# Compressed keys of layer 1: two full-array fp32r products of high and low rows in place of two fp32 products of 15 rows

## Chip, cores and metric

The kernel runs on 1 core of one Trainium2 chip. The metric is the device time of one launch in microseconds (us), lower is better. The time of a kernel is the median of several runs; one further execution is taken with the hardware profiler, and all rows below are of that one.

## What is computed

The reference is two layers of a decoder on one sequence of 256 positions with 1024 channels. Each layer is RMS norm, attention, output projection, residual; then a SwiGLU block with 2816 hidden channels; then a gated per-layer embedding. Layer 0 has two kinds of local attention and isn't touched here. Layer 1 has 16 query heads in 4 groups, each group with its own keys and values, and three branches that are summed with sigmoid gates:

```python
s = jnp.einsum('bghsd,bgcd->bghsc', qg, kc).astype(F32) * ATTN_SCALE + tabg[:, :, _rel_bucket(dc)].astype(F32)
p_cmp, _ = _masked_softmax(s, dc >= 0)
o_cmp = jnp.einsum('bghsc,bgcd->bghsd', p_cmp.astype(vc.dtype), vc)
...
o = (gates[..., 0:1] * o_cmp.reshape(B, H, S, hd) + gates[..., 1:2] * o_slc.reshape(B, H, S, hd)
     + gates[..., 2:3] * o_win.reshape(B, H, S, hd))
```

Here `kc` and `vc` are the compressed keys and values: windows of 32 positions with a stride of 16, each put through a small two-layer network. A sequence of 256 gives 15 of them for each group. The change concerns the product `o_cmp`, of the weights over these 15 compressed keys (`p_cmp`) with their values.

## The kernel before

Everything is fp32 in memory. The large products are made of fp32r products: each weight tile is split by ScalarE (a rounded copy `hi`, L135) and VectorE or GpSimd (the rest `lo`, L137), the activations likewise into the x tiles, `X[0]` and `X[1]`, which hold for each of 8 rows of 128 channels a high and a low part of 256 positions. Three products (high by high, low by high, high by low) stand for one of fp32. The attention of both layers works with plain fp32 for the softmax weights and the values.

TensorE's and the load queue's (SP) instructions run in the order in which the program writes them; the other engines' order is left to the framework's scheduler. The program's order comes from a planner. Every product adds its price to a clock `clk` (`mm`, L148 to L153): the larger of moving and stationary columns over 2400 us, times 4 for fp32, times 0.56 if the product has only 64 stationary columns or 64 rows. Side jobs (generators) give out their next step once the clock has reached their due time, between two chunks of the large products (`tick`, `side_step`). The constants in `KN` are due times and distances in this clock.

In layer 1 these side jobs run beside the projections for q, k and v, then `ple_proj` (tile `pa`) and the output projection (`oc`):

- `compress` (from L935) makes the compressed keys and values. Its second step copies the hidden values of each group into 4 blocks of 32 columns (L989), so that the product with the second weight leaves the values `VC` four times along the partitions, one copy at rows 0, 32, 64 and 96.
- `cmp_scores(b)`, once for each half `b` of the heads (two groups), makes the scores against the 15 compressed keys (`cs`), the softmax (L1035 to L1044), and writes the weights into `PC` with 32 columns for a head, of which 15 are used (L1046, two VectorE products). Four transposes (`pcp`) and one ScalarE copy (L1053) bring them to `PCT`, with 4 heads along the partitions.
- `attend` drives, for each half, the steps A (scores `s`, softmax with L498, L1082, L1083 to L1087), B (transposes `t`, copies to `pt`, L1097 and L1099) and C. C(k) is run 4 times for each half, once for a pair of heads: the heads `j` of the two groups.

C opens with the two products of the compressed branch, one for each head `e` of the pair, 15 rows and 64 columns of the stationary operand each:

```python
for e in range(2):
    mm(o[64 * e:64 * e + 64, 0:256], VC[32 * j:32 * j + 15, gs[e], :],
                     PCT[32 * j:32 * j + 15, gs[e], :], start=True, stop=False)
```

Then it adds the eight fp32 products of the other two branches with the values (`o<-pt`), and `o_evac` (L494, L495) brings the tile `o` into row `h0 // 2 + k` of `X[1]`, high part by ScalarE and low part by VectorE. The output projection reads `X[1]` two rows at a time (`out_proj`). When it is done, its result goes into `h` (L518) and, normalised, into a new `X[0]` (L412, L413).

`PCT` shares memory with `KCV`, the projected inputs of `compress`. `X[0]` holds the input of layer 1's projections and isn't read after the last of them. The memory of `X[1]` holds the first weight of `compress` (`w1`) until that has been used.

Of the kernel before, what the change touches and what calls it, by code (L numbers as in the profile page):

```python
# [39 lines left out]
def trunk(ctx: ExitStack, tc: tile.TileContext, a, out):  # L40
# [108 lines left out]
    def mm(o, l, r, start, stop):  # L149
        n, m = int(np.prod(r.shape[1:])), l.shape[-1]  # L150
        f = 1.0 if l.dtype == F32R else 4.0
        clk[0] += f * max(n, m) / 2400 * (0.56 if m == 64 or l.shape[0] == 64 else 1.0)
        nc.tensor.matmul(o, l, r, start=start, stop=stop)  # L153
# [703 lines left out]
    PCT = big2[:, 1536:2560].rearrange("p (g s) -> p g s", g=4)  # L857
    VC = big2[:, 2560:2816].rearrange("p (g d) -> p g d", g=4)
    G = big2[:, 2816:2912].rearrange("p (t h b) -> p t h b", t=2, h=16)
# [77 lines left out]
    def compress(idr):  # L937
# [44 lines left out]
        atvv = atv.rearrange("p (g r c) -> p g r c", g=4, r=4)  # L982
# [5 lines left out]
        for g in range(4):  # L988
            nc.vector.tensor_copy(atvv[:, g, :, 0:15], p[:, 64 + g * 15:79 + g * 15][:, None, :].to_broadcast([128, 4, 15]))  # L989
# [19 lines left out]
        for e in range(2):  # L1009
            ph, kh, gh = p[64 * e:64 * e + 64], KCT[64 * e:64 * e + 64, :, e], g[64 * e:64 * e + 64]  # L1010
            pv = bass.AP(tensor=ph.tensor, offset=ph.offset + 15 * e, ap=[ph.ap[0], [30, 2], [1, 16]])
            nc.scalar.activation(kh[:, :, 0, :], pv, AF.Identity, scale=gh)
            nc.vector.scalar_tensor_tensor(kh[:, :, 1, :], pv, gh, kh[:, :, 0, :].bitcast(F32), op0=OP.mult, op1=OP.subtract)
        ev["kc"] = clk[0] + 0.8

    def cmp_scores(b):
        if b == 0:
            nc.gpsimd.memset(PC, 0.0)
# [25 lines left out]
        nc.vector.tensor_tensor(l, l, G[:, :, 8 * b:8 * b + 8, 0], op=OP.mult)  # L1044
        for t in range(2):
            nc.vector.tensor_tensor(PC[:, t, :, 0:15], sc[:, t], l[:, t, :, None].to_broadcast([128, 8, 15]), op=OP.mult)  # L1046
# [6 lines left out]
        nc.scalar.activation(PCT[:, 2 * b:2 * b + 2, :], p.rearrange("p (a s) -> p a s", a=2), AF.Copy)  # L1053
        ev[f"cmp{b}"] = clk[0] + 0.8

    def attn1(h0):
# [45 lines left out]
        def C(k):  # L1102
# [3 lines left out]
            for e in range(2):  # L1106
                mm(o[64 * e:64 * e + 64, 0:256], VC[32 * j:32 * j + 15, gs[e], :],
                                 PCT[32 * j:32 * j + 15, gs[e], :], start=True, stop=False)
# [34 lines left out]
    new_x(1)  # L1143
# [77 lines left out]
```

## Time and profile before

| | |
|---|---|
| median of 3 runs | 715.0 us (711.7 to 715.34) |
| profiled execution, its own time | 709.85 us |
| its span, first to last instruction | 708.0 us |
| TensorE (PE) busy | 691.6 us, 98% |
| VectorE (DVE) busy | 509.2 us, 72% |
| ScalarE (ACT) busy | 411.6 us, 58% |
| GpSimd (POOL) busy | 179.4 us, 25% |

In the trace, times are counted from the span's start. An instruction is named by its engine, its line in the kernel, its operation and the tiles it writes and reads; "x4" is a number of instructions that stand in one row. A matmul's duration holds its way through the array, and consecutive ones overlap, so what a matmul costs in a row of many is read from the distance between starts. An fp32 matmul leaves two records. A note in brackets at the end of a row is the time that the engine stood idle before it, and what ended that. The chain of work that ended last is followed back from the last instruction: at each step to what released it, or to the instruction before it on its engine.

### The profile page before, as it was taken

What the parts mean: (1) busy time and instruction counts of PE and PEld (TensorE: products, weight loads), DVE (VectorE), ACT (ScalarE), POOL (GpSimd) and SP (SyncE); (2) the same over time, 40 slices, a digit from 0 to 9 for tenths busy, and PEclk for the clock granted to TensorE, in tenths of its full rate; (3) what the DMA queues carried; (4) which work ended last, traced back from release to release, by engine and by line L of the source; (5) the groups of instructions that cost most, each with busy time, mean ns of one, the idle gap of its engine ahead of it and who ended that gap; (6) DMA issues with size and microseconds to landing.
All of it is one profiled execution on the core that took longest, in us unless ns stands there. A gap on an engine that the chain in (4) does not pass through costs nothing.

```text
span 708.0 us, 12005 instructions
## 1 busy us (share of the span) xinstructions
PE 691.6 (98%) x4394; PEld 597.2 (84%) x4394; DVE 509.2 (72%) x973; ACT 411.6 (58%) x761; POOL 179.4 (25%) x287
## 2 busy tenths in 40 slices
PE   8999999999999999999999999998999999999996
PEld 6887789898888888899878867787988888888896
DVE  6669674878867765767876887766697778757465
ACT  7557685655665653554654777776465656645342
POOL 1353100242132220001163544341232321310010
PEclk9999999999999999999999999999999999999999
DMA  8956424556556565547763253622567555654611
GB/s 313 322 177 220 161 96 125 149 174 209 183 175 218 172 205 199 185 152 230 216 218 121 87 150 97 173 61 90 150 185 226 165 198 169 217 191 167 209 60 60
DMA packets 69931, 121.66 MB, mean 172 GB/s; under 512 B 5488, under 2 KB 17648, under 8 KB 69872
## 3 DMA queue, kind: packets, MB, share of 16 engines
q1 hardware_dynamic: 69872, 120.89, 53.6%
q8 instruction: 34, 0.56, 0.3%
q14 instruction: 25, 0.20, 0.1%
HBM read 119.83 MB, written 1.05 MB: 171 GB/s over the span
## 4 chain that ended last, share of the span: by engine, by line
PE 79%; DVE 7%; ACT 5%; POOL 4%; issue 3%; DMA 2%; SPq 0%; DVEq 0%; ACTq 0%; POOLq 0%
PE ua L153 17%; PE ga L153 17%; PE da L153 17%; PE oc L153 5%; PE ic L153 5%; PE pc L153 5%; DVE lo L137 3%; PE o L153 3%; ACT hi L135 2%; PE q L153 2%; PE s L153 2%; PE t L157 1%; PE v L153 1%; DMA raw<-in_w_in_nsa_dram 1%; PE pa L153 1%
## 5 line engine op out<-in xcount | busy, mean ns | idle before, releaser
L137 DVE TENSOR_TENSOR lo<-raw,hi 128x1024 fp32r<-128x1024 f32 (+2 forms) x218 | 265.7, 1230 | 106.4 <-ACT hi L135 106.1
L135 ACT ACTIVATE hi<-raw 128x1024 fp32r<-128x1024 f32 (+4 forms) x231 | 223.8, 987 | 159.3 <-PE da L153 50.7
L153 PE MATMUL ua<-x,hi 128*128 128x512 f32 (+1 forms) x384 | 96.1, 375 | 0.0
L153 PE MATMUL ga<-x,hi 128*128 128x512 f32 x352 | 92.9, 395 | 2.3 <-DVE h L518 1.8
L153 PE MATMUL da<-big,hi 128*128 128x512 f32 x352 | 89.6, 393 | 0.0
L153 PE MATMUL ic<-hi,x 128*128 128x512 f32 (+2 forms) x256 | 78.6, 376 | 0.1
L153 PEld LDWEIGHTS ua<-x,hi 128*128 128x128 f32 x384 | 65.9, 189 | 8.7
L153 PEld LDWEIGHTS ga<-x,hi 128*128 128x128 f32 x352 | 61.6, 189 | 12.8 <-DVE h L518 2.6
L153 PEld LDWEIGHTS da<-big,hi 128*128 128x128 f32 x352 | 62.7, 189 | 10.7
L601 POOL TENSOR_TENSOR th<-th,rfb 128x512 f32<-128x512 f32 x22 | 28.5, 1295 | 127.1 <-DVE th L600 127.1
L425 POOL TENSOR_TENSOR sum<-sum,sqj 128x512 f32<-128x512 f32 x12 | 17.1, 1422 | 171.2 <-ACT sqj L423 171.1
L153 PE MATMUL ua<-x,lo 128*128 128x256 f32 x352 | 57.1, 282 | 0.0
L153 PEld LDWEIGHTS ua<-x,lo 128*128 128x128 f32 x352 | 52.7, 189 | 5.1
L153 PEld LDWEIGHTS ga<-x,lo 128*128 128x128 f32 x352 | 51.0, 189 | 5.5
L153 PEld LDWEIGHTS ic<-hi,x 128*128 128x128 f32 x256 | 46.6, 188 | 10.2 <-issue 2.1
L153 PEld LDWEIGHTS da<-big,lo 128*128 128x128 f32 x352 | 49.1, 190 | 4.2
L153 PE MATMUL ga<-x,lo 128*128 128x256 f32 x352 | 52.5, 281 | 0.0
L153 PE MATMUL da<-big,lo 128*128 128x256 f32 x352 | 50.3, 282 | 0.0
L153 PE MATMUL oc<-x,hi 128*128 128x256 f32 x256 | 48.5, 289 | 0.1
L153 PE MATMUL ic<-lo,x 128*128 128x512 f32 (+2 forms) x128 | 46.9, 366 | 0.0
L153 PE MATMUL pc<-x,hi 128*128 128x256 f32 x256 | 46.6, 284 | 0.0
L610 POOL TENSOR_TENSOR th<-us,th 128x512 f32<-128x512 f32 x20 | 36.3, 1817 | 37.9 <-DVE us L568 37.9
(199 smaller groups left out, 1131.5 us busy)
## 6 DMA issues: line engine op xcount, KB each, us to landing
raw<-in_w_ffn_gate_dram SPq DMA_DIRECT2D x44, 512.0 KB, 3.7
raw<-in_w_ffn_up_dram SPq DMA_DIRECT2D x44, 512.0 KB, 4.4
raw<-in_w_ffn_down_dram SPq DMA_DIRECT2D x44, 512.0 KB, 3.8
raw<-in_w_in_ab_dram SPq DMA_DIRECT2D x23, 512.0 KB, 5.8
raw<-in_w_ple_gate_dram SPq DMA_DIRECT2D x16, 512.0 KB, 4.0
raw<-in_w_in_nsa_dram SPq DMA_DIRECT2D x12, 512.0 KB, 4.8
raw<-in_w_out_ab_dram SPq DMA_DIRECT2D x8, 512.0 KB, 3.3
raw<-in_w_in_nsa_dram SPq DMA_DIRECT2D x16, 256.0 KB, 3.8
```

Source lines behind the costliest of these rows:

```text
L135: nc.scalar.activation(hi[:, x:x + m], r[:, x:x + m], AF.Copy)
L137: e.tensor_tensor(lo[:, x:x + m], r[:, x:x + m], hi[:, x:x + m].bitcast(F32), op=OP.subtract)
L153: nc.tensor.matmul(o, l, r, start=start, stop=stop)
L157: nc.tensor.transpose(o, i, ident if idn is None else idn)
L425: e.tensor_tensor(st["sum"], st["sum"], j, op=OP.add)
L601: nc.gpsimd.tensor_tensor(v2(th), v2(th), r2(), op=OP.mult)
L610: nc.gpsimd.tensor_tensor(y, x, y, op=OP.mult)
```

## The change

The weights of the 15 compressed keys and their values are split into high and low parts, as the large products' operands are. The high and the low part of a head's weights lie side by side, at columns 0 to 14 and 16 to 30 of its 32, so that after the transposes a head has 32 rows: 15 high, one zero, 15 low, one zero. The values stand eight times along the partitions (blocks of 16) instead of four times, so that both the high and the low rows of a head meet the same values. For each pair of heads a stationary operand of 128 rows is built in which all but the pair's rows are zero: columns 0 to 63 hold the values of the first group in the rows of the pair's first head, columns 64 to 127 those of the second group in the rows of the second head. To that end `PC` is ordered by pairs (`p (j e) c`), and a mask `msk`, one column for each block of 32 rows, multiplies `VC` (`vc_blocks`). C then opens with two products over all 128 rows and 128 columns, with the high and with the low part of the values.

The new tiles have no memory of their own. For the first half of the heads they lie in rows 5 to 7 of `X[1]`, for the second in rows 5 to 7 of `X[0]` (`cmp_homes`). `new_x(1)` moves from the code after the projections into the end of `compress`.

```diff
-    PCT = big2[:, 1536:2560].rearrange("p (g s) -> p g s", g=4)
     VC = big2[:, 2560:2816].rearrange("p (g d) -> p g d", g=4)
+    PCR, VCR, PHR = {}, {}, {}
+    msk = small("msk", (128, 4))
+    nc.vector.tensor_reduce(msk, ident.rearrange("p (s c) -> p s c", c=32), axis=AX.X, op=OP.add)
+
+    def cmp_homes(b):
+        x = X[1 - b].rearrange("p k e s -> p k (e s)")
+        PCR[b] = x[:, 7].rearrange("p (q s) -> p q s", q=2)
+        VCR[b] = x[:, 6].rearrange("p (l n) -> p l n", l=2)
+        PHR[b] = x[:, 5, 0:240]
+
+    def vc_blocks(b):
+        w = wk_tile("vcw")[:, 0:256].rearrange("p (j e d) -> p j e d", j=2, e=2)
+        for j in range(2):
+            nc.vector.tensor_tensor(w[:, j], VC[:, 2 * b:2 * b + 2, :], msk[:, 2 * j:2 * j + 2][:, :, None].to_broadcast([128, 2, 64]),
+                                    op=OP.mult)
+        wf = w.rearrange("p j e d -> p (j e d)")
+        nc.scalar.activation(VCR[b][:, 0], wf, AF.Copy)
+        nc.vector.tensor_tensor(VCR[b][:, 1], wf, VCR[b][:, 0].bitcast(F32), op=OP.subtract)
...
-        atvv = atv.rearrange("p (g r c) -> p g r c", g=4, r=4)
+        atvv = atv.rearrange("p (g r c) -> p g r c", g=4, r=8)
...
-            nc.vector.tensor_copy(atvv[:, g, :, 0:15], p[:, 64 + g * 15:79 + g * 15][:, None, :].to_broadcast([128, 4, 15]))
+            nc.vector.tensor_copy(atvv[:, g, :, 0:15], p[:, 64 + g * 15:79 + g * 15][:, None, :].to_broadcast([128, 8, 15]))
...
+        new_x(1)
+        cmp_homes(0)
+        vc_blocks(0)
         ev["kc"] = clk[0] + 0.8

     def cmp_scores(b):
+        if b:
+            cmp_homes(1)
...
+        nc.vector.tensor_tensor(sc, sc, l[:, :, :, None].to_broadcast([128, 2, 8, 15]), op=OP.mult)
+        nc.scalar.activation(PHR[b], w[:, 0:240], AF.Copy)
+        ph = PHR[b].bitcast(F32).rearrange("p (t e j c) -> p t e j c", t=2, e=2, j=4)
+        sv = w[:, 0:240].rearrange("p (t e j c) -> p t e j c", t=2, e=2, j=4)
         for t in range(2):
-            nc.vector.tensor_tensor(PC[:, t, :, 0:15], sc[:, t], l[:, t, :, None].to_broadcast([128, 8, 15]), op=OP.mult)
+            pc = PC[:, t].rearrange("p (j e) c -> p e j c", e=2)
+            nc.vector.tensor_tensor(pc[:, :, :, 16:31], sv[:, t], ph[:, t], op=OP.subtract)
+            nc.scalar.activation(pc[:, :, :, 0:15], ph[:, t], AF.Copy)
+        if b:
+            vc_blocks(b)
         yield KN["cmp"]
...
-        nc.scalar.activation(PCT[:, 2 * b:2 * b + 2, :], p.rearrange("p (a s) -> p a s", a=2), AF.Copy)
+        nc.scalar.activation(PCR[b], p.rearrange("p (a s) -> p a s", a=2), AF.Copy)
...
-            for e in range(2):
-                mm(o[64 * e:64 * e + 64, 0:256], VC[32 * j:32 * j + 15, gs[e], :],
-                                 PCT[32 * j:32 * j + 15, gs[e], :], start=True, stop=False)
+            b = h0 // 8
+            for l in range(2):
+                mm(o[:, 0:256], VCR[b][:, l, 128 * (j % 2):128 * (j % 2) + 128], PCR[b][:, j // 2], start=l == 0, stop=False)
...
-    new_x(1)
```

## Rows read from the trace of the kernel before

**Rows 1.** The page, part 2: granted TensorE clock in 40 slices

```profile
PEclk9999999999999999999999999999999999999999
```

**Rows 2.** Busy time by stretch: PE, PEld, DVE, ACT, POOL, clock, DMA

```profile
397.50:437.30 39.80, 36.75 (x255) 28.50 (x254) 32.43 (x119) 30.14 (x91) 17.56 (x29) 1.00 0.38 100
437.30:452.35 15.05, 14.12 (x113) 11.07 (x113) 11.17 (x52) 9.99 (x33) 6.05 (x9) 1.00 0.69 194
452.35:485.60 33.25, 33.02 (x278) 25.64 (x278) 21.40 (x89) 22.68 (x71) 9.53 (x13) 1.00 0.27 80
```

**Rows 3.** Timeline of PE around the first C: start, us, instruction

```profile
419.74 0.40 PE L153 MATMUL pa<-px,hi 128*128 128x256 f32 x2
419.98 0.28 PE L153 MATMUL pa<-px,lo 128*128 128x256 f32 x1
420.18 0.65 PE L153 MATMUL o<-big 15*64 15x256 f32 x4
420.76 1.52 PE L153 MATMUL o<-pt,big 128*64 128x256 f32 x16
```

**Rows 4.** Busy time of PE in C's eight opening pairs, summed

```profile
sum 4.63, PE 4.62; mean PE 0.58
```

**Rows 5.** The chain that ended last, by time: start, us, work

```profile
428.15 1.18 POOL rs_tq L396
...
441.69 2.03 PE o L153 x20
...
445.84 0.77 ACT big L1082 x4
...
452.35 2.10 PE o L153 x20
...
482.64 2.05 PE o L153 x20
```

**Rows 6.** Groups by shape, 340 to 495 us, DVE, ACT: busy, mean ns

```profile
L1039 DVE TENSOR_TENSOR csw<-csw,cm 128x240 f32<-128x240 f32 x2 | 0.8, 404 | 0.0
...
L989 DVE COPY at<-atp 128x60 f32<-128x60 f32 x4 | 0.6, 210 | 0.0
...
L435 DVE TENSOR_TENSOR sum<-sum 128x256 f32<-128x256 f32 x1 | 0.4, 424 | 0.0
...
L135 ACT ACTIVATE hi<-raw 128x256 fp32r<-128x256 f32 x4 | 1.5, 420 | 1.0 <-issue 1.0
...
L1040 ACT ACTIVATE csw<-csw 128x240 f32<-128x240 f32 x2 | 0.8, 396 | 0.2 <-DVE csw L1039 0.2
...
L977 ACT ACTIVATE big<-big 128x128 f32<-128x128 f32 x1 | 0.3, 312 | 0.0
```

**Rows 7.** Timeline of DVE, first half of the heads, then the second

```profile
409.52 1.56 DVE L1046 TENSOR_TENSOR big<-csw,cl 128x120 f32<-128x120 f32 x2
...
413.97 1.23 DVE L137 TENSOR_TENSOR lo<-raw,hi 128x1024 fp32r<-128x1024 f32 x1 [0.86 <-ACT hi L135]
...
446.74 0.45 DVE L1046 TENSOR_TENSOR big<-csw,cl 128x120 f32<-128x120 f32 x2
...
447.97 0.69 DVE L137 TENSOR_TENSOR lo<-raw,hi 128x512 fp32r<-128x512 f32 x1 [0.70 <-ACT hi L135]
```

**Rows 8.** Timeline of POOL at the same two places

```profile
408.98 1.77 POOL L137 TENSOR_TENSOR lo<-raw,hi 128x512 fp32r<-128x512 f32 x1 [4.97 <-ACT hi L135]
...
447.43 2.86 POOL L1087 TENSOR_SCALAR big<-big,rl 128x128 f32<-128x128 f32 x4 [8.19 <-DVE rl L1085]
```

**Rows 9.** Timeline of ACT, second half of the heads

```profile
447.30 1.16 ACT L135 ACTIVATE hi<-raw 128x512 fp32r<-128x512 f32 x2 [0.69 <-issue]
449.10 0.51 ACT L1082 ACTIVATE big<-big,nm 128x256 f32<-128x256 f32 x1 [0.63 <-DVE nm L498]
```

**Rows 10.** Timeline of PE: the transposes of the weights, both halves

```profile
413.14 0.60 PE L157 MATMUL pcp<-ident,big 128*128 128x128 f32 x4
...
450.54 0.60 PE L157 MATMUL pcp<-ident,big 128*128 128x128 f32 x4
```

## The prediction

> **What bounds the kernel now.** I read the page's slices first, for the clock. TensorE is granted 90% of its clock or more in every slice [rows 1] and 1.00 in the stretches that matter here [rows 2], the higher of its two levels, 2.4 GHz; so a product costs the same wherever it stands, and nothing here is won or lost by the clock. Next came the busy time by stretch, cut where the attention of layer 1 changes character [rows 2]. From 397.5 to 437.3 us TensorE is busy 36.75 of 39.80 us, from 437.3 to 452.35 us 14.12 of 15.05, and from 452.35 to 485.6 us 33.02 of 33.25. So the last stretch is bound by TensorE alone, while the first two hold 3.05 + 0.93 = 4.0 us in which it stands idle. Then came the chain that ended last [rows 5], for the question whether TensorE also sets the time where the changed products stand. It does so from 452.35 us on. Before that the chain changes hands: at 428.15 us it runs over GpSimd while TensorE has other work, at 441.69 us it is on TensorE, from 445.84 us on ScalarE, and back on TensorE at 452.35 us. VectorE and ScalarE are no bound by their sums (11.17 and 9.99 of 15.05 us in the middle stretch), but they carry the chain there.
>
> **The change, part by part.**
>
> *The products.* Step C of a pair of heads opens with two fp32 products of 15 rows, which leave four records. The first starts at 420.18 us, and the products with the values (o<-pt) follow at 420.76: 0.58 us [rows 3]. Over the eight pairs it is 4.63 us, 0.58 each [rows 4]. In their place come two fp32r products of 128 rows, 128 stationary columns and 256 moving ones. That is the shape and type of the pa products just before: two start at 419.74 us and the next at 419.98, so 0.12 us each with their weight loads [rows 3]. The new pair costs 0.24 us, and C gets shorter by 0.58 - 0.24 = 0.34 us, eight times 2.7 us. One thing the rows leave open is the change from a full-array fp32r product to an fp32 one on part of the array. From the last pa product to the first 15-row one it took 0.20 us instead of 0.12, so 0.08 more. I take it that this gap then stands in front of o<-pt instead; if it falls away a pair saves 0.42 us, if it comes twice 0.26. All eight then lie between 2.1 and 3.4 us.
>
> *What of it is on the path.* Six of the eight groups are pieces of the chain: those at 441.69 and 452.35 us, three between there and the last, and the last at 482.64 [rows 5]. The first two, the one at 420.18 us and the next, are not: the chain passes through ScalarE, VectorE and GpSimd then, as at 428.15 us; what they save becomes a longer wait of TensorE a few us on. So 6 x 0.34 = 2.0 us counts (1.6 to 2.5).
>
> *More work for VectorE and ScalarE, once for each half of the heads.* Before, two VectorE products wrote the weights of the compressed keys. After, one 128x240 product takes their place (0.40 us, as L1039 [rows 6]), ScalarE rounds it (0.40, as L1040), VectorE subtracts twice (the pair at 446.74 us has that size, 0.45 [rows 7]) and ScalarE copies the high parts twice (0.31 each, as L977). The masked values add two VectorE products of 128x128 (0.46, taken from the same pair), a ScalarE copy of 128x256 (0.42, as L135 of that shape) and a VectorE subtraction (0.42, as L435). VectorE: 0.40 + 0.45 + 0.46 + 0.42 less the 0.45 removed is 1.28 us. ScalarE: 0.40 + 0.62 + 0.42 is 1.44 us.
>
> For the first half there is cover. The old pair ends at 409.52 + 1.56 = 411.08 us [rows 7], and the transposes of the weights follow at 413.14 [rows 10]: 2.06 us of room, where the longer way (0.40 + 0.40 + 0.45 us, with the copies beside it) takes some 0.8 more than the old pair's 0.45, hand-overs apart. VectorE also waits 0.86 us before 413.97 us for a ScalarE split [rows 7]. I count nothing; without that cover the weights' own share, 0.40 us of VectorE (0.40 + 0.45 - 0.45) and 1.02 of ScalarE, 1.4 us in all, is the end.
>
> For the second half the place is worse. The work falls behind 446.74 us, where the chain is on ScalarE and VectorE until 452.35. The idle time there is 0.70 us on VectorE before 447.97 [rows 7], and 0.69 and 0.63 us on ScalarE before 447.30 and 449.10 [rows 9]. VectorE's 1.28 less 0.70 leaves 0.58 us; ScalarE's 1.44 less 1.32 leaves 0.12. The weights are wanted only by the transposes at 450.54 us [rows 10], and the masked values not before the first C of that half, which comes behind the one at 452.35 us; so some of this can go later, at no cost. I take 0.5 us. The lower end is 0, the upper one all 2.7 us in line.
>
> These VectorE instructions read both inputs from SBUF, and here the trace has a warning. The same pair of products took 1.56 us at 409.52 and 0.45 us at 446.74 [rows 7]; during the slow one GpSimd was in a subtraction of 1.77 us that began at 408.98 [rows 8]. So an overlap with GpSimd can cost 1.1 us, and GpSimd runs for 2.86 us from 447.43 on [rows 8], just where the second half's additions go.
>
> The Trainium skill, SBUF — State Buffer, section "Who interferes with whom", has a rule that speaks against this change: a VectorE instruction with two SBUF inputs and a GpSimd instruction that reads SBUF exclude each other, and the later one is held until the earlier is through. By that rule the slow pair above is no accident, the trace agrees (1.56 against 0.45 us), and each of the six such instructions in a half can be held or can hold GpSimd; by the rows alone, one hold of 1.1 us is what has been seen. With two holds in line the sum below would be +0.7 us instead of -1.5.
>
> *Small parts.* The four copies of the hidden values write 120 columns for 60; they take 0.21 us each [rows 6], so at most four times that more, 0.84 us, if time goes with width; but a 120-wide product of the pair at 446.74 us takes 0.23 [rows 7], so it is nearer nothing. The mask is one VectorE reduction of 128x128, under the 0.40 us of a 240-wide pass, and wants nothing but the identity. Both lie before 397 us, on an engine that is not the chain there for long: I take 0, the ends are 0 and 1.2 us. The homes in the two x tiles add no wait that ends late: rows 5 to 7 of one are overwritten by pairs 5 to 7 of the outputs, after the C at 452.35 us which reads them last, and the other's last readers are the projections before the second half's scores. No DMA is added or moved; new_x(1) only allocates, a little earlier.
>
> *The written-out order.* The planner prices a product by its columns: the two fp32 ones 2 x 4 x 256/2400 x 0.56 = 0.48 us, the new two 2 x 256/2400 = 0.21. Its clock thus runs 0.27 us shorter for every C, and steps that are due by that clock come later among the instructions. From the first C on, the order of TensorE's stream can shift by a few products. TensorE's idle 4.0 us of the first two stretches is what can be won or lost by that; I take 0, between -2 and +2.
>
> **Sum.** -2.0 + 0.5 = -1.5 us. The profiled execution has a span of 708.0 and a time of 709.85 us; it would become 708.35. The median of the runs shown is 715.0, 5.15 us above it, and the three runs lie 3.6 us apart. I set the difference against the median: 713.5 us.
>
> **Rivals.**
> *VectorE and ScalarE take over (slower).* The place is the second half, 446.7 to 452.35 us. For it speaks that the chain is already on these engines, and that GpSimd is running; against it, idle time on both and inputs that are wanted late. If all 2.7 us stand in line with two holds of 1.1 us, and only the four C after 452.35 us give their 0.34, the result is 2.7 + 2.2 - 1.4 = +3.5 us; with the first half's 1.4 us uncovered as well it is +4.9, 719.9 us. It decides for slower as soon as the added wait on the way to 452.35 us passes 5.0 us (1.4 + 3.6).
> *The order falls luckily (faster).* All eight C count, 2.7 us, and the shifted order takes 2 of the 4.0 us of waits away: -4.7, 710.3 us. For it: waits stand there to be lost. Against it: nothing in the change aims at them.
> *No gain.* What TensorE saves comes back as waiting because the softmax steps on ScalarE and VectorE set when the next products can start: 0, 715.0 us. For it: the hand-overs of the chain before 452.35 us; against it, 33.02 of 33.25 busy after.
>
> **How the numbers follow.** About 0.5% or 3.6 us is what a measurement of this kernel can tell from no change. The forecast of -1.5 us has a chance of 0.36, no gain 0.22, the lucky order 0.24, VectorE and ScalarE 0.18. The first two lie within 3.6 us: same 0.58, faster 0.24, slower 0.18. The likeliest case has its own range of 711.6 to 715.5: from all 3.4 us gained to 0.5 lost (1.6 gained against 2.1 of the 2.7 in line). The range of 8 in 10 takes in the lucky order and the near part of the slow rival, down to 709.5 and up to 717.5 us.
>
> **What would show it right or wrong.** Right: fp32r products of 128x256 in front of o<-pt, 0.24 us for the two, TensorE as busy as before after the fourth C, and a fourth C that waits for ScalarE at most half a us longer. Wrong: 0.3 us or more for one product; a wait for the transposes of the weights; the pair of new subtractions drawn out to over 1 us beside GpSimd; or waits of TensorE in the attention of layer 1 which differ from the 4.0 us by more than 2.

## The result, and the profile after

The changed kernel takes 709.33 us (median of 13 runs, 707.82 to 711.95). The kernel before, run beside it, takes 711.87 us (13 runs, 709.77 to 716.61). The ratio of the runs is 0.9947, with a 95% interval of 0.9923 to 0.9971: a gain of about half a per cent. The forecast was 713.5 us with a range of 709.5 to 717.5; the result lies 0.17 us below it. The forecast difference was -1.5 us, the measured one is -2.5 by the two medians.

Of the 13 runs of before, seven lie at 709.8 to 711.9 us and six at 715.0 to 716.6, and two of the three shown ahead of the prediction are of the latter; the experiments show what parts them.

The busy time by stretch of the changed kernel answers to [rows 2]; the cuts are at the second half's compressed scores and at the fourth C, which comes 2.9 us earlier now, at 449.49 us (452.35 before). The last line comes from a finer cut behind the attention.

```profile
397.50:437.43 39.93, 36.65 (x253) 28.56 (x252) 33.13 (x133) 30.75 (x98) 16.98 (x32) 1.00 0.40 101
437.43:449.49 12.06, 11.43 (x97) 9.81 (x96) 10.64 (x41) 9.00 (x30) 3.66 (x5) 1.00 0.92 239
449.49:485.00 35.51, 35.05 (x292) 28.55 (x291) 22.90 (x93) 23.67 (x74) 11.57 (x14) 1.00 0.26 75
...
492.00:496.00 4.00, 4.00 (x16) 3.50 (x15) 4.00 (x8) 2.04 (x4) 0.06 (x1) 0.57 0.31 84
```

TensorE's idle time is 3.28 + 0.63 + 0.46 = 4.4 us (4.2 before): it did not shrink. The last line is new. From 492 to 496 us the clock was granted at 0.57 on the mean, which is the lower level of 1.2 GHz for most of the stretch. The page's row of slices shows nothing of it: it is a 9 in every slice, as in [rows 1], since a slice is 17.7 us and 4 us at 0.57 leave 0.90 in it.

The timeline of TensorE at the first C answers to [rows 3].

```profile
420.89 0.28 PE L153 MATMUL pa<-px,lo 128*128 128x256 f32 x1
421.01 0.40 PE L153 MATMUL o<-x 128*128 128x256 f32 x2
421.34 1.52 PE L153 MATMUL o<-pt,big 128*64 128x256 f32 x16
```

From the last pa product to o<-pt it is 421.34 - 420.89 = 0.45 us; before it was 420.76 - 419.98 = 0.78 us. So a pair saves 0.33 us, against 0.34 in the prediction. The gap stands in front of o<-pt now, as supposed there.

The next lines are the first half's preparation of the shares, as the softmax weights are called from here on (VectorE, GpSimd, ScalarE, TensorE), answering to [rows 7, 8, 10].

```profile
408.64 1.78 POOL L137 TENSOR_TENSOR lo<-raw,hi 128x512 fp32r<-128x512 f32 x1 [5.12 <-ACT hi L135]
409.19 1.50 DVE L1071 TENSOR_TENSOR csw<-csw,cl 128x240 f32<-128x240 f32 x1
...
410.78 0.40 ACT L1072 ACTIVATE x<-csw 128x240 fp32r<-128x240 f32 x1 [0.74 <-DVE csw L1071]
...
413.58 1.06 ACT L135 ACTIVATE hi<-raw 128x1024 fp32r<-128x1024 f32 x1 [2.40 <-DMA raw<-in_w_out_nsa_dram]
414.54 0.48 ACT L1078 ACTIVATE big<-x 128x120 f32<-128x120 f32 x2
...
414.88 0.74 PE L157 MATMUL pcp<-ident,big 128*128 128x128 f32 x4 [1.88 <-ACT big L1078]
```

The two copies of the high parts could have run at 411.2 us. In ScalarE's order they stand behind a split of weights that waits 2.40 us for its DMA, so they start at 414.54 and the transposes wait 1.88 us for them. The same split had much the same wait in the profile of before, where no such copy stood behind it:

```profile
412.88 1.06 ACT L135 ACTIVATE hi<-raw 128x1024 fp32r<-128x1024 f32 x1 [2.49 <-DMA raw<-in_w_out_nsa_dram]
```

In the second half the same work meets no such split:

```profile
444.79 0.41 DVE L1071 TENSOR_TENSOR csw<-csw,cl 128x240 f32<-128x240 f32 x1
446.21 0.40 ACT L1072 ACTIVATE x<-csw 128x240 fp32r<-128x240 f32 x1
446.64 0.50 ACT L1078 ACTIVATE big<-x 128x120 f32<-128x120 f32 x2
446.64 0.48 DVE L1077 TENSOR_TENSOR big<-csw,x 128x120 f32<-128x120 f32 x2
...
451.27 0.66 PE L157 MATMUL pcp<-ident,big 128*128 128x128 f32 x4
```

Here the copies run beside the subtractions and the transposes wait for nothing. The product L1071 took 1.50 us in the first half beside a GpSimd subtraction and 0.41 in the second without one.

The 1.88 us are TensorE's longest wait from 400 to 495 us. The next is one of 1.79 us behind the first gate products of the feed-forward (`ga`); here after the change, and below it the same products before:

```profile
488.92 0.86 PE L153 MATMUL ga<-x,hi 128*128 128x512 f32 x3
491.57 1.94 PE L153 MATMUL ga<-x,hi 128*128 128x512 f32 x5 [1.79 <-DVE h L518]
493.31 1.91 PE L153 MATMUL ga<-x,lo 128*128 128x256 f32 x8
495.01 2.32 PE L153 MATMUL ga<-x,hi 128*128 128x512 f32 x8
```

```profile
493.64 1.45 PE L153 MATMUL ga<-x,hi 128*128 128x512 f32 x5 [1.79 <-DVE h L518]
494.93 1.10 PE L153 MATMUL ga<-x,lo 128*128 128x256 f32 x8
495.87 2.00 PE L153 MATMUL ga<-x,hi 128*128 128x512 f32 x8
```

The feed-forward's first products start at 488.92 us, 2.07 us earlier than in the profile of before (490.99). The whole span is only 0.5 us shorter, 707.5 against 708.0. The other 1.5 us went right behind the 1.79 us wait for the output projection's copy into `h`, where the clock fell: by the distance between starts, eight products of 256 columns took 1.70 us from 493.31 on, 0.21 each, and 0.94 us, 0.12 each, before. The wait is as long in the profile of before, and there the clock stayed at 1.00.

### The profile page after: what moved, and what is told of

Its sections match the earlier page's. It is cut to its first block, busy times and chain, and to the rows that moved or that the text cites. A ratio compares the mean times of both kernels' runs of the same rounds, so it can differ in the third digit from the quotient of the medians.

```text
span 707.5 us, 11993 instructions
## 1 busy us (share of the span) xinstructions
PE 691.6 (98%) x4378; PEld 600.2 (85%) x4378; DVE 513.8 (73%) x982; ACT 413.0 (58%) x769; POOL 179.7 (25%) x287
## 3 DMA queue, kind: packets, MB, share of 16 engines
HBM read 119.83 MB, written 1.05 MB: 171 GB/s over the span
## 4 chain that ended last, share of the span: by engine, by line
PE 81%; DVE 7%; ACT 3%; issue 3%; POOL 3%; DMA 2%; SPq 0%; DVEq 0%; ACTq 0%; POOLq 0%
PE ga L153 18%; PE ua L153 17%; PE da L153 17%; PE oc L153 6%; PE ic L153 5%; PE pc L153 5%; DVE lo L137 3%; PE o L153 3%; PE v L153 2%; PE t L157 2%; PE s L153 2%; PE q L153 2%; PE pa L153 1%; DMA raw<-in_w_in_nsa_dram 1%; ACT hi L135 1%
```

## The experiments

Every run of the experiments has a mean granted clock of TensorE; beside each median stands the mean of it over the runs, and in brackets the number of runs. A mean of 0.998 needn't cost anything: in some executions the clock falls after TensorE's last product, while the outputs are written (run 10's profile: 0.72 at 704 to 706 us and 0.50 at 706 to 708, with TensorE at rest since 703).

**1 and 2. The two kernels again, as a scale.**

> The kernel before, unchanged, with the granted clock of every run. Theory A (the work alone explains the difference): the clock is 1.00 in all runs, the times lie close together and the median is 1.5 to 2.5 us above that of the changed kernel. Theory B (a drop of TensorE's clock behind the wait between output projection and feed-forward, which the profile of the changed kernel shows once, from 492.4 to 495.6 us, takes part in the difference): the runs differ by some us, and those with a lower mean clock are the longer ones.

> The changed kernel, unchanged, on the same chip. Theory A: 0.3% under the kernel before, about 2.1 us, as the start of the feed-forward moved from 490.99 to 488.92 us. Theory B: runs with a clock of 1.00 are near 706 us of span, those with 0.997 near 707.5, and the difference to the kernel before depends on how many of its runs have the lower clock.

Measured: before 712.37 us (12; 710.32 to 717.39), clock 0.9954; changed 709.72 us (12; 707.80 to 712.11), clock 0.9975, ratio to before 0.9955 (0.993 to 0.998). The kernel before also ran beside each set of experiments, 125 times in all (one execution of 1728 us left out). By the clock they are: 22 at 1.000 with a median of 710.4 us, 37 at 0.997 to 0.999 with 710.65, 39 at 0.993 to 0.996 with 713.6, and 27 at 0.992 or less with 716.5. At clock 1.000 the changed kernel takes 707.8 to 708.7 us (five runs, median 708.0). So it gains 2.4 us at full clock, and the spread of before up to 716 us goes with the clock, as theory B had it.

The profiled execution of the first run had a clock of 0.990 and a span of 715.6 us. Theory B put the fall behind the feed-forward's wait; here there is none at that place, but two earlier ones. Windows (columns as in [rows 2]) and timeline of TensorE around the longer one:

```profile
440.00:444.00 4.00, 3.71 (x24) 3.31 (x25) 1.91 (x10) 2.09 (x9) 2.22 (x4) 0.79 0.03 6
444.00:448.00 4.00, 4.00 (x20) 2.83 (x21) 3.02 (x13) 1.06 (x1) 0.00 (x0) 0.50 0.95 250
448.00:452.00 4.00, 4.00 (x26) 2.87 (x23) 2.10 (x10) 0.99 (x4) 0.00 (x0) 0.50 1.06 274
```

```profile
440.29 0.96 PE L153 MATMUL s<-big,big 64*128 64x512 f32 x6 [1.08 <-DVE pt L1097]
441.18 2.57 PE L153 MATMUL cs<-kct,big 128*128 128x64 f32 x16
...
446.43 1.12 PE L153 MATMUL o<-big 15*64 15x256 f32 x4
```

and the same place in the profile of [rows 2]:

```profile
437.32 0.97 PE L153 MATMUL s<-big,big 64*128 64x512 f32 x6 [1.07 <-DVE pt L1097]
438.21 1.96 PE L153 MATMUL cs<-kct,big 128*128 128x64 f32 x16
```

TensorE waits 1.08 us, does six score products on half of the array's rows and sixteen short ones of compressed scores, and has the lower clock until about 452.5 us; the fp32 pair takes 1.05 us there (o<-pt follows at 447.48) for 0.58 at full clock. In the profile of [rows 2] the wait before the same products is as long (1.07 us), and the clock stayed up. So the same program has the fall in some executions and not in others. The shorter fall of run 1 is at 416 to 424 us (0.81 and 0.77 in windows of 4 us), behind a wait of 2.30 us before the second block of transposes.

**3. New products, old order.** The planner is told the old price, so that TensorE's order is exactly that of before.

```
 def C(k):
+    clk[0] += 2 * (4 * 0.56 - 1) * 256 / 2400
```

> The changed kernel with the planner's clock advanced by 2 x (4 x 0.56 - 1) x 256/2400 = 0.26 us more in each C, so that TensorE's instructions keep the order that they have in the kernel before. If the saved time of the products is the whole story, the time is that of the changed kernel (ratio to before 0.997). If the shifted order brought the gain, this kernel is near the kernel before (0.999 to 1.001). If the shifted order costs, it is faster than the changed kernel (0.995).

Measured: 715.94 us (12), clock 0.9930, ratio to before 1.0039 (1.0017 to 1.0061). That is above all that was expected: with the old order the whole gain is lost, and more. Its profile has the fall at the same place, behind a 1.06 us wait, and shows what the wait is made of:

```profile
437.55 1.27 POOL L137 TENSOR_TENSOR lo<-raw,hi 128x512 fp32r<-128x512 f32 x1 [5.88 <-ACT hi L135]
437.60 1.24 DVE L1119 TENSOR_TENSOR rl<-rl,big 128x4 f32<-128x4 f32 x1
...
438.76 0.54 DVE L1131 COPY pt<-t 128x384 f32<-128x384 f32 x1
...
439.36 0.96 PE L153 MATMUL s<-big,big 64*128 64x512 f32 x6 [1.06 <-DVE pt L1131]
```

A product of four columns takes 1.24 us on VectorE beside GpSimd's subtraction (the same form took 0.16 us at 408.30 in the changed kernel's profile), the copy behind it is late, and TensorE waits for the bank that the copy empties. The kernel before has this too: 1.24 us for the same product at 435.56, beside a GpSimd subtraction that began at 435.51.

**4. The added work alone, in the old order**, with the old fp32 products:

```
+        nc.scalar.activation(PHR[b], w[:, 0:240], AF.Copy)
...
+            nc.vector.tensor_tensor(PC[:, t, :, 16:31], sc[:, t], ph[:, t], op=OP.subtract)
+            nc.scalar.activation(PC[:, t, :, 0:15], ph[:, t], AF.Copy)
+        if b:
+            vc_blocks(b)
```

> The kernel before with the changed kernel's preparations on VectorE and ScalarE added (mask, masked values split in two, weights split in two), and its own two fp32 products, which here use only the high part of the weights; the low parts and the masked values are made and not used. The price of the added work alone. By the prediction 0 to 0.5 us (ratio 1.000 to 1.001). If the copies of the high parts stand behind a split that waits for a load, as in the changed kernel, the transposes of the first half wait up to 1.9 us and the time rises by up to that, 1.002 to 1.003. If VectorE and ScalarE set the time, 2.7 us or more, 1.004.

Measured: 712.91 us (12), clock 0.9961, ratio 1.0003 (0.9977 to 1.0029). The transposes of the first half wait 1.5 us for the copies here too, as the second expectation had it, while the ratio is that of the first; its interval takes in both, so the run doesn't give the price.

**5. The new order alone**, with old products and preparations:

```
 def C(k):
+    clk[0] -= 2 * (4 * 0.56 - 1) * 256 / 2400
```

> The kernel before with its own fp32 products and its own preparations; only TensorE's order is that of the changed kernel. Theory 'the order keeps the clock up': the idle wait before s and cs near 440 us is gone, the mean granted clock over the runs rises from the 0.995 of before to the 0.9975 of the changed kernel, and the time falls by that alone, about 1.2 us, to 711 to 712 beside 712.9 of before. Theory 'only the shorter products count': the clock and the time stay as before, 712.5 to 713.5.

Measured: 712.21 us (12), clock 0.9957, ratio 0.9984 (0.9953 to 1.0015): inconclusive, and the mean clock did not rise as the first theory wanted. The 1.1 us wait before s is gone, but 1.5 us before the second block of transposes is left, and 1.8 before the first gate products.

**6. The new products in the new order without the preparations:**

```
-            pc = PC[:, t].rearrange("p (j e) c -> p e j c", e=2)
...
+            nc.vector.tensor_tensor(PC[:, t, :, 0:15], sc[:, t], l[:, t, :, None].to_broadcast([128, 8, 15]), op=OP.mult)
...
+        nc.gpsimd.memset(VCR[0].rearrange("p l n -> p (l n)").bitcast(F32), 0.0)
```

> The changed products in the changed order with the preparations of before; the low parts and the values' blocks stay at zero, so the compressed branch leaves nothing in the output. If the added preparations cost something on the path (the 1.8 us wait for the copies at the first half's transposes), this is 0.5 to 1.5 us faster than the changed kernel: 708.3 to 709.3, and that wait is below 1 us. If the wait costs nothing because other waits take its place, it is the same as the changed kernel, 709.5 to 710.

Measured: 708.28 us (10), clock 0.9974, ratio 0.9927 (0.990 to 0.9954). At the same clock as the changed kernel (0.9975, on another chip) it is 709.72 - 708.28 = 1.4 us faster, or 2.0 by the two ratios to before (0.9955 and 0.9927); the wait for the copies is gone. That is what the preparations cost by this pair of runs, more than the prediction's 0.5 us and at or above the upper end of what was expected of the run.

**7. More columns in the compressed scores, in the old order.** The first product of each pair gets wider, and the order of the pairs changes with it (`t` outside `j`, lines not shown), so that the surplus columns are overwritten:

```
-                        mm(pv[:, t, j].rearrange("p e l c -> p (e l c)"), q, KCT[:, b].rearrange("p e l c -> p (e l c)"), start=True, stop=False)
+                        x = 64 * (4 * t + j)
+                        n = min(192, 512 - x)
+                        mm(cs[:, x:x + n], q, KW[:, b, 0:n], start=True, stop=False)
```

> The changed products in the order of before, as in the third run, with one more edit: the first of each pair of compressed score products streams 192 columns of keys instead of 64 (the other columns are overwritten by the next product). If what the array does right after its idle wait near 440 us decides whether the clock falls there, the stretch of 0.50 at 440 to 450 us becomes rare, the mean clock rises from 0.993 to 0.996 or more and the time falls from 715.9 to about 713 or less. If only the idle wait decides, clock and time stay at 0.993 and 715 to 717.

Measured: 714.30 us (12), clock 0.9938, ratio 1.0005 (0.9981 to 1.003). Between the two theories. The profiled execution kept its clock at 440 us and lost it at 452 to 459, behind a 1.2 us wait. What TensorE does behind the wait is at most part of it; whether the transposes ahead of it take part was not tried.

**8. The high parts written in place**, which takes the late copies away:

```
-        nc.scalar.activation(PHR[b], w[:, 0:240], AF.Copy)
...
-            nc.vector.tensor_tensor(pc[:, :, :, 16:31], sv[:, t], ph[:, t], op=OP.subtract)
-            nc.scalar.activation(pc[:, :, :, 0:15], ph[:, t], AF.Copy)
+            nc.scalar.activation(pc[:, :, :, 0:15].bitcast(F32R), sv[:, t], AF.Copy)
+            nc.vector.tensor_tensor(pc[:, :, :, 16:31], sv[:, t], pc[:, :, :, 0:15], op=OP.subtract)
```

> The changed kernel, but ScalarE writes the rounded high parts straight into the block that is transposed, so the two later copies of 0.48 us a half are gone; TensorE's order is the same. If the first half's transposes are late by these copies behind the split that waits for a DMA, the 1.8 us wait there falls to 0.9 or less and the time to 708.5 to 709.3. If the split itself is the last, wait and time stay, 709.5 to 710.

Measured: 711.22 us (12), clock 0.9943, ratio 0.9973 (0.9947 to 1.000). A miss for both theories. The 1.88 us wait is gone, as wanted; 1.29 us before a later transpose stands in its place, and the median is above the changed kernel's 709.72 (on another chip; the intervals of the two ratios, 0.9973 and 0.9955, overlap). Its mean clock is lower, and its profile has the fall behind the gate products' wait:

```profile
492.00:496.00 4.00, 4.00 (x15) 3.57 (x16) 4.00 (x8) 2.39 (x4) 0.39 (x1) 0.59 0.35 104
```

After eight runs the theory was that idle waits of TensorE let the clock fall. The next four put work into the waits: products of the identity with itself, which write a strip that nobody reads, issued just before the instruction that waits.

```
+    def fill(o, n):
+        for _ in range(n):
+            nc.tensor.matmul(o, ident, ident, start=True, stop=True)
...
         u = wide([st_tile("ua") for _ in range(2)]) + packed([st_tile("ua")])
+        fill(u[0][0][:, 0:128], 7 * l)
```

The second part is the place before the gate products; the others look alike.

**9. The wait before s filled, new products in the old order.**

> The changed products in the order of before (third run), and one more edit: five products of the identity with itself, 1.06 us of TensorE, go into an unused strip of a tile right before the s that waits 1.06 us for a copy at 439 us. Nothing reads them. Theory 'an idle wait lets the clock fall': the stretch at 0.50 at 440 to 448 us goes in most executions, the mean granted clock over the runs rises from 0.993 to 0.996 or more, and the time falls from 715.9 to 713.5 or less although TensorE has 1.06 us more to do. Theory 'the clock has to do with the products behind the wait, or with nothing here': clock 0.993, and 715.5 to 717.

Measured: 714.58 us (12), clock 0.9947, ratio 1.0023 (0.9997 to 1.0048). Timeline of TensorE, and windows:

```profile
439.08 1.28 PE L178 MATMUL t<-ident 128*128 128x128 f32 x10
441.23 1.96 PE L153 MATMUL cs<-kct,big 128*128 128x64 f32 x16
...
453.26 0.52 PE L157 MATMUL t<-ident,p 128*128 128x128 f32 x3 [0.88 <-DVE nm L504]
454.99 1.08 PE L157 MATMUL pcp<-ident,big 128*128 128x128 f32 x4 [1.22 <-ACT pt L1141]
```

```profile
440.00:444.00 4.00, 4.00 (x34) 3.43 (x33) 2.51 (x13) 2.63 (x10) 2.25 (x4) 1.00 0.02 6
444.00:448.00 4.00, 4.00 (x39) 3.27 (x39) 4.00 (x15) 1.86 (x4) 0.00 (x0) 1.00 0.98 252
452.00:456.00 4.00, 1.91 (x10) 1.15 (x9) 3.13 (x9) 3.00 (x12) 2.71 (x4) 0.85 0.59 202
456.00:460.00 4.00, 4.00 (x23) 2.79 (x24) 2.40 (x15) 2.25 (x9) 0.25 (x1) 0.50 0.38 122
```

The clock stays at 1.00 where it had been 0.51, and falls behind the next two waits instead (0.88 and 1.22 us). One filled wait wasn't enough: the median is 1.4 us below run 3, 1.1 us by the two ratios since the chips differ, and it lies between the two theories.

**10 to 12. All longer waits filled**, in the changed kernel, in the one with high parts in place, and in the kernel before.

> The changed kernel with such products in three idle waits: two (0.43 us) before the first half's scores, seven (1.49 us) before the first half's four transposes, seven before the first gate products of the feed-forward. If idle waits let the clock fall, no stretch below full clock is left, the mean clock is 0.999 or more, and the time is that of the changed kernel at full clock, 708.0 to 708.7 beside 709.7. If they don't, clock 0.9975 and 709.5 to 711.

> The kernel with the high parts written in place (eighth run, clock 0.994 and 711.2 us) with such products before the first half's scores (two), in the 1.29 us wait inside the first transposes of probabilities (five) and before the first gate products of the feed-forward (seven). If idle waits let the clock fall, the mean clock is 0.998 or more and the time 707.5 to 708.7, the fastest so far. If they don't, clock 0.994 and 711 to 712.5.

> The kernel before, its products and order as they were, with such products in four idle waits: one before the first half's scores, five in the wait between the first two blocks of transposes (1.29 us, 415 us), five before the s that waits 1.07 us at 437 us, seven before the first gate products. If idle waits let the clock fall, its clock rises from 0.995 to 0.998 or more and its time falls from 712.9 to 710.5 to 711.3, and the changed kernel with its waits filled is then 2.0 to 2.8 us below it: the change's own part without the clock. If they don't, clock 0.995 and 712.5 to 714.

Measured: changed and filled 709.25 us (12; 708.38 to 710.91), clock 0.9983, ratio to before 0.9959 (0.9935 to 0.9982); high parts in place and filled 708.32 (12; 707.24 to 708.85), clock 0.9991, ratio 0.9944 (0.9922 to 0.9966); before and filled 710.55 (12; 709.76 to 711.28), clock 0.9992, ratio 0.9971 (0.9945 to 0.9997). Eighteen products that compute nothing hold the clock of the kernel before: no run is above 711.3 us, while 66 of its 125 unfilled runs, all at a clock of 0.996 or less, have medians of 713.6 and 716.5. The windows of the filled kernel before, over the places where the clock had fallen:

```profile
412.00:424.00 12.00, 11.06 (x81) 8.75 (x80) 8.93 (x36) 9.25 (x27) 4.08 (x7) 1.00 0.60 149
436.00:452.00 16.00, 15.37 (x129) 12.77 (x128) 13.06 (x52) 10.67 (x32) 6.96 (x10) 1.00 0.62 168
488.00:500.00 12.00, 11.77 (x84) 10.74 (x84) 11.12 (x16) 9.25 (x16) 2.67 (x2) 1.00 0.26 70
```

So filling the waits keeps the clock, and the theory stands. Not all went as expected: the changed kernel filled came out 0.5 us above its bound with a mean clock below the 0.999 expected, and only 1.3 us below before filled, where 2.0 to 2.8 was expected. Its timeline of TensorE shows a reason:

```profile
413.73 1.72 PE L178 MATMUL pcp<-ident 128*128 128x128 f32 x14
415.70 0.74 PE L157 MATMUL pcp<-ident,big 128*128 128x128 f32 x4 [0.25 <-ACT big L1087]
...
417.55 0.52 PE L157 MATMUL t<-ident,p 128*128 128x128 f32 x3 [0.45 <-DVE nm L504]
418.94 0.52 PE L157 MATMUL t<-ident,p 128*128 128x128 f32 x3 [0.88 <-ACT x L1097]
419.39 0.63 PE L153 MATMUL s<-big,big 64*128 64x256 f32 x6
```

From the start of the last product ahead of the wait (413.50) to the s behind the transposes it is 5.89 us. In the changed kernel's own profile the same way, with the 1.88 us wait in it, takes 4.94 us (412.61 to 417.55). The fill products fit into the wait, but 0.95 us more stands behind them. What differs there is ScalarE's order, which is the scheduler's: its copy of the transposed shares comes after two of the four softmax steps that follow the transposes in the changed kernel (416.03), and after all four here (418.20). So filling a wait is no pure test of the clock; it can move other engines' work.

**13 to 15. The three parts of the change, with the waits filled.** New products and preparations in the old order; old ones in the new order; new products, old preparations, new order.

> The changed products and preparations in the order of before, with products that nobody reads in five idle waits: two before the first half's scores, six before the first half's transposes of shares, five before the s at 439 us, five before the second half's transposes of shares, seven before the first gate products. Theory 'the old order lost the gain through the clock alone': at a mean clock of 0.998 or more the sum of the parts is left, 710.5 less 2.1 for the products and more by 0.9 for the preparations: 709.0 to 709.8. Theory 'the old order also makes TensorE wait, because it was written for longer products': clock as high, but 711 to 712.5, above the filled kernel before at 710.5.

> The products and preparations of before in TensorE's new order, with products that nobody reads in three idle waits (one before the first half's scores, five in the 1.54 us wait between the first two blocks of transposes, seven before the first gate products). If the order by itself gains time with the clock held, 709.2 to 709.9, that is 0.6 to 1.3 below the filled kernel before (710.55). If the order was worth only the clock, 710.3 to 710.9.

> The changed products in the new order with the preparations of before (the compressed branch leaves nothing in the output), waits filled as in the run before. If the eight pairs save what the prediction summed (six on the path at 0.34 us, 2.0 us), it is 1.8 to 2.3 below that run, 707.0 to 707.8; if other work takes part of it, less than 1.5 below. The difference to the filled changed kernel (709.25) and to the one with high parts in place (708.32) is what the preparations cost: 1.5 to 2 and 0.7 to 1.2.

Measured: 712.55 us (12), clock 0.9980, ratio 1.0003 (0.9982 to 1.0025); 709.55 (12), clock 0.9991, ratio 0.9965 (0.9947 to 0.9982); 707.11 (6), clock 0.9987, ratio 0.9928 (0.9902 to 0.9955). Expected were 709.0 to 709.8 or 711 to 712.5 for the first, and the second theory holds, 0.05 us above its range; the second and third came out as their first theories had it, with the preparations just above the upper ends. The medians with the waits filled, all from one chip, with 13 to 25 fill products each, as many as the waits of the kernel asked for:

| filled, us | old order | new order |
|---|---|---|
| old products and preparations | 710.55 | 709.55 |
| new products, old preparations | not run | 707.11 (6 runs) |
| new products and preparations | 712.55 | 709.25 |
| the same, high parts in place | not run | 708.32 |

The new order gives -1.0 us with the old products (the two sets of runs overlap, 709.8 to 711.3 and 708.8 to 710.6). The new products then give -2.44, and the preparations take +2.14 back, or +1.21 with the high parts in place. The unfilled runs at clock 1.000 are a second reading: 710.4 us for before (22 runs), 709.7 for the new order (one run), 707.6 for the products without preparations (two) and 708.0 for the changed kernel (five). By these few the order gives -0.7, the products -2.2, and the preparations cost 0.5. So order and products are alike in both readings, and the price of the preparations is not: 0.5 to 2.1 us, the upper end with the moved copy of run 10 in it.

In the old order the new products and preparations cost 2.0 us even with the clock at 0.998. Run 3 without fill products agrees: its nine runs at 0.993 to 0.996 have a median of 715.8 us, the 39 of before 713.6. The profile of run 13 shows TensorE waiting there, in the first half as in the others, but also in the second:

```profile
452.13 0.52 PE L157 MATMUL t<-ident,p 128*128 128x128 f32 x3 [0.86 <-DVE nm L504]
452.51 1.38 PE L178 MATMUL pcp<-ident 128*128 128x128 f32 x10
453.88 0.71 PE L157 MATMUL pcp<-ident,big 128*128 128x128 f32 x4
```

That wait of 0.86 us, and the 1.22 us which fill products cover behind it, are absent in the new order, where the transposes at 451.27 us wait for nothing. My reading is that an order written for pairs of 0.58 us puts too little between steps when the pairs take 0.24; no run varies that distance by itself.

## Why the prediction was wrong

**The base, and the clock: the step that failed.** The prediction said that "nothing here is won or lost by the clock", and set its difference "against the median: 713.5 us". Both rest on one profiled execution at clock 1.000 (709.85 us) and three runs, two of them at 715 us. The clock of these three is not on record, but the later runs of the same kernel show what parts such times: 710.4 us at 1.000, 716.5 at 0.992 or less, 710.55 once the waits are filled, and all 33 of the 125 that took 715 us or more had 0.993 or less. So the 5.15 us between median and profiled execution go with the clock, as far as can be told, and the base was some 3 us too high: with the 711.87 us of the 13 runs the same -1.5 us would have given 710.4, inside the range. Against the profiled execution the prediction gave 708.35, and the changed kernel takes 708.0 at that clock. A median 5 us above the profiled execution should have been asked for its cause first.

The Trainium skill, TensorE: Matmul & The Clock Gate, section "Part 1: The HAM clock gate (the "warmup" mystery)", states that the clock follows how busy TensorE has been, and that throttled is the default from which activity releases it. The runs agree: the clock fell to 0.50 behind waits of 1.08, 2.30, 1.79 and 1.22 us, and none of the six profiles with all of the longer waits filled (runs 10 to 15) has a stretch of 4 us below 1.00 while TensorE works. What no run settles is why an execution falls behind a wait and another doesn't, and why four profiles (runs 2, 3, 6 and 9) have a fall at 400 to 408 us, where only 0.42 to 0.58 us of waiting and the short compressed scores stand in front.

**The products.** 0.34 us a pair was predicted, 0.33 is read from the timeline, and with the clock held the eight give -2.44 us in the new order. "Six of the eight" was a little short: 2.44 / 0.33 is 7.4, and in the changed kernel's chain, which answers to [rows 5], seven of the C are pieces, from the second on:

```profile
429.73 1.69 PE o L153 x18
...
480.91 1.71 PE o L153 x18
```

**The written-out order.** "I take 0, between -2 and +2": it is worth -1.0 us by itself (run 14 against 12, the sets of runs overlap), and more than that, it decides whether the products gain at all: the same new kernel takes 709.25 us in the new order and 712.55 in the old. Taking the term as zero was the second failing step, though its bounds held. Nothing in the change aims at this, but the price of a product is an input of the order, so a cheaper product comes with an order of its own.

**The added work.** "For the first half there is cover... I count nothing" failed as well. The room on VectorE was there; the cover broke on ScalarE's queue, where the copies stand behind a split that waits 2.40 us for a DMA. The trace of before had that wait (2.49 us at 412.88), and the prediction looked at VectorE's rows alone there. In the second half, for which 0.5 us was counted, the transposes wait for nothing; its masked values were made at 439.7 to 441.0 us, well ahead of the place behind 446.74 us that the prediction gave them. The sum was +0.5 with ends of 0 and 4.1 (1.4 + 2.7); the cost is 0.5 us at clock 1.000 by few runs, 1.4 at the changed kernel's mean clock, and 2.1 with fill products. So the place was wrong, and whether the size was stays open.

**The sum** of -1.5 us is near the measured -1.3 with filled waits by terms that balance, -2.4 - 1.0 + 2.1 for -2.0 + 0 + 0.5, which is luck; it is 0.9 short of the -2.4 at full clock, where the parts are -0.7 - 2.2 + 0.5. The two measured differences are 1.1 us apart, about as much (0.95 us) as the changed kernel's first half was longer in its profile with fill products (run 10); that this is the cause is read from one profile each and was not tried by itself.

**The hold by GpSimd.** A hold of 1.1 us was feared in the second half. None came there; the one of the first half (1.50 us for L1071 against 0.41) stood in the kernel before at the same place (1.56 us, [rows 7]), so the change added none. The prediction's rule from the Trainium skill, SBUF — State Buffer, "Who interferes with whom", that a VectorE instruction with two SBUF inputs contends with a GpSimd instruction that reads SBUF, agrees with both, and with the product of four columns in run 3 (1.24 us). Two holds in line, the slow rival's condition, did not come.

**The rivals.** "The order falls luckily" was nearest in time (710.3 us) and right that the order gains. Its time is luck: -4.7 us from a base that was some 3 us too high, where -2.5 was measured. "VectorE and ScalarE take over" is nearest to what happens in the old order: TensorE waits for them in both halves, and the time is 712.55 us with the waits filled and 715.94 without. Of the signs that the prediction named, the products of 0.24 us a pair and a TensorE that is busy after the fourth C (35.05 of 35.51 us) are there, and one of the wrong ones, the wait for the transposes of the weights. The new subtractions were not drawn out (0.44 and 0.48 us for the pair), and the waits of the first two stretches stayed near the 4.0 us (3.28 + 0.63 = 3.9).

**A version that may be faster.** High parts in place and waits filled: 708.32 us, 0.9 below the filled changed kernel on the same chip, its slowest run (708.85) below the changed kernel's medians of 709.33 and 709.72. Those were not measured beside it, and the ratios to before (0.9944 against 0.9947 and 0.9955) don't part them. What it does give is a spread of 1.6 us instead of 4.

## What to carry to other kernels

Before a difference is predicted, ask which clock the profiled execution and the runs had, stretch by stretch of a few us; the slices of a page hide a fall of 4 us. Where the runs spread and the clock with them, products without a purpose in TensorE's waits of 1 to 2 us are a cheap test and a cheap cure (18 of them took before from 711.3 to 710.55 us, and its highest run from 717.0 to 711.3 on that chip); a wait that costs little by the sum can cost more by the clock: the runs of before with a lower clock are 3 to 6 us longer. Such products can also move the work of other engines, as in run 10, so the profile has to be read again with them in. When an instruction gets cheaper in a kernel whose order is written by a planner, change price and instruction separately once: here the cheaper product gains only with the order that its price writes.

## What the hardware showed that was not expected

A wait taken away needn't make a kernel faster: run 8 lost the 1.88 us wait, its mean clock came out at 0.9943 where the changed kernel has 0.9975, and its median 1.5 us higher (on another chip, with overlapping ratios, so slower is not shown); with its waits filled the same kernel has the lowest median of those that do the whole work. And a product of four columns took 1.24 us on VectorE beside a GpSimd subtraction, and so set off a TensorE wait of 1.06 us, behind which the clock fell in run 3; in the kernel before, the same wait (1.07 us) let it fall in one profile and not in another.
